# mLSTM gate rows on 32 partitions, worked out beside GLA, in a hybrid mixer kernel

## The chip, the cores and the metric

The kernel runs on one core of a Trainium2 chip. The metric is the device time of one execution in microseconds, taken as the median of several executions. TensorE (PE) multiplies, VectorE (DVE) and GpSimd (POOL) work elementwise, ScalarE (ACT) does functions and casts, and SyncE (SP) issues nearly all DMAs. Each engine works through its own instructions in order and waits on semaphores for the others.

## The reference, cut to what matters

The whole program is a hybrid mixer block (three branches: GLA, mLSTM and S5, then a merge and a SwiGLU feed-forward) followed by an MLA and RG-LRU block, for 1024 tokens of width 1024 in float32. The change touches the gates of the mLSTM branch:

```python
def mlstm_memory(q, k, v, i_pre, f_pre):
    log_f = jax.nn.log_sigmoid(f_pre.astype(f32))
    ...
        b = jnp.cumsum(lfi, axis=-1)                      # inside a chunk
        a_inter = b + m_prev[..., None]
        d_intra = jnp.where(causal, b[..., :, None] - b[..., None, :] + ii[..., None, :], -jnp.inf)
        m_t = jnp.maximum(a_inter, jnp.max(d_intra, axis=-1))
        w_inter = jnp.exp(a_inter - m_t)
        scores = jnp.einsum('bhtd,bhsd->bhts', qi, ki) * jnp.exp(d_intra - m_t[..., None])
        ...
        h = num / jnp.maximum(jnp.abs(den), jnp.exp(-m_t))[..., None]
        w_key = jnp.exp(b[..., -1:] - b + ii - m_new[..., None])
```

There are 4 heads of key width 64 and value width 128, and the mixer also holds `y_gla = rms_norm(o_gla) * silu(gr)`, `y_ml = sigmoid(mo) * h_ml` and `y_s5 * sigmoid(y_s5 @ s5_glu_w + s5_glu_b)`, whose products stand next to the change in the program. Six rows of modulation come from `silu(c) @ ada_w + ada_b`.

## The kernel before, in words

Every float32 product is split into a high and a low part and done as three matmuls (`mm3`), with operands of 128 rows and 256 or 512 columns. Weights come by one DMA (`wr`), a cast on ACT (`wh`) and a difference on DVE (`wl`). `e()` gives one of four general 128x1028 buffers: loads, gate results and stores all pass through these four. PSUM tiles are `psg` (big products) and `psc` (small ones).

Code is written as generators that yield an estimated delay. A small driver (`spawn`, `push`, `drive`) runs them by a clock of its own and so fixes the order in which instructions are written; after that a scheduler with a timeline of its own reorders them on each engine. Pools lie on two stacks of the on-chip memory, left and right. Where a pool is opened on space that another one has left, each new tile waits for the last users of whatever tile lay there before (`reuse_waits="tile"`).

The order around the change is this:

- GLA stage: `gla_pair` for two pairs of heads runs beside the products `in_ml` (mLSTM's q and k, written to `d_mq`) and `in_v(1)` (its v). `ada_rest` is not yet there in program order, but the scheduler moves its first loads and sums forward into this stage.
- Gate rows: `ml_rows` loads the pre-activations of the gates as two 4x1024 tiles, `mr_i` and `mr_f` (one partition for each head, all 1024 steps along it), and makes from them log-sigmoid, sums inside a chunk, the running maximum by one scan over 1024 steps, and the rows that the mLSTM needs, in two 128x1024 tiles printed as `r`. `ml_core` transposes one of them in 8 pieces to columns (`becol`, `wkcol`, `encol`) and exponentiates two; `sel` is a matrix that picks a row and spreads it over 128 partitions.
- mLSTM stage: `ml_core` works in four blocks (two pairs of heads, two halves of the time). A block loads q, k, v (one buffer each), spreads the gate rows by `r,sel` and a mask `mneg`, takes `D` by Exp, and does `q,k`, `v,kT`, `Sz,qt` and `v,P` and the transposes of `P`. Beside it run `in_gr` (the GLA gate, `psg<-ah,wh` and so on), `s5_glu` (loads `e<-d_sy`, eight DMAs for each of four pieces, cast to `gh`, low part `gl`, and products `gh,wh` and so on), `in_mo`, and `proj(2)`.
- `ada_rest` goes through eight groups. A group clears the accumulator `ada0` on POOL, loads a piece of bias into it, then for 8 weights loads one (three buffers `ada1` to `ada3`) and adds it on DVE, sums over partitions with a matmul by `ones`, and stores a row to `d_rows`.
- Projections: `load_yb` loads a branch's output and splits it in `yb0` (high, ACT) and `yb1` (low, DVE); `proj` makes eight 128x1024 tiles, copied out of `psg` by ACT (`e<-psg`) and stored to `d_p`. `proj(0)` asks at its sixth tile for the load of `proj(1)`'s operand, into a pool `yb2` that is opened after mLSTM and `ada_rest` have ended, on the space that they leave.

Of the kernel before, what the change touches and what calls it, by code (L numbers as in the profile page):

```python
# [51 lines left out]
class Kernel:  # L52
# [1105 lines left out]
    def ml_rows(self, p):  # L1158

        nc = self.nc  # L1160
        t = lambda n: p.tile([4, 1024], F32, name="mr_" + n)
        r1 = self.mrow.tile([128, 1024], F32, name="r1")
        r2 = self.mrow.tile([128, 1024], F32R, name="r2")
        nc.gpsimd.memset(r1, 0.0)
        nc.gpsimd.memset(r2.bitcast(F32), 0.0)
        f, i, a = t("f"), t("i"), t("a")
        nc.sync.dma_start(i, self.d_misc[32:36])
        nc.sync.dma_start(f, self.d_misc[64:68])
        self.ts(i, i, self.co["ifb"][0:4, 0:1], op0=ALU.add)
        self.ts(f, f, self.co["ifb"][0:4, 1:2], op0=ALU.add)  # L1170
        self.log_sigmoid(a, f)
        b, m = t("b"), a
        self.local_sums(b, f, 4)
        nc.vector.tensor_tensor_scan(out=m, data0=f, data1=i, initial=0.0, op0=ALU.add, op1=ALU.max)
        m_be, m_ka, m_nm = r1[0:4], r1[32:36], r1[64:68]
        self.m_cols, self.m_rows = r1, r2
        c8 = lambda x: x.rearrange("p (c n) -> p c n", c=8)
        m_a, aw = t("ma"), f
        self.tt(m_a, b, m, ALU.subtract)
        self.tt(m_be, i, b, ALU.subtract)  # L1180
        self.ts(m_nm, m, -1.0)
        nc.vector.tensor_copy(aw[:, 0:128], m_a[:, 0:128])
        self.tt(c8(aw)[:, 1:], c8(m_a)[:, 1:],
                c8(m)[:, 0:7, 127:128].to_broadcast([4, 7, 128]), ALU.add)
        self.tt(c8(m_ka), c8(m_be), c8(m_a)[:, :, 127:128].to_broadcast([4, 8, 128]), ALU.add)

        for o, x in ((0, m_a), (64, aw)):
            h = p.tile([4, 1024], F32R, tag="mr_h", name="mr_h")
            nc.vector.tensor_copy(h, x)
            self.tt(r2[o + 32:o + 36], x, h.bitcast(F32), ALU.subtract)  # L1190
            nc.scalar.copy(r2[o:o + 4], h.bitcast(F32))

    def ml_core(self, p1, p2):
        nc, A = self.nc, self.A
        sel = p1.tile([128, 6, 128], F32R, name="sel")
# [3 lines left out]
        for o in (0, 32, 64, 96):  # L1199
            nc.sync.dma_start(sf[o:o + 4], sv)  # L1200
        nc.gpsimd.tensor_copy(sel, sf)
        yield 16.0

        be = p1.tile([128, 8, 4], F32, name="becol")
        wk = p1.tile([128, 8, 4], F32, name="wkcol")
        en = p1.tile([128, 8, 4], F32, name="encol")
        for g in range(2):
            pcol = self.psc()
            for c in range(4):
                self.tr(pcol[:, c * 128:c * 128 + 128], self.m_cols[:, (4 * g + c) * 128:(4 * g + c) * 128 + 128])  # L1210
            pv = pcol.rearrange("p (c n) -> p c n", c=4)
            cs = slice(4 * g, 4 * g + 4)
            nc.vector.tensor_copy(be[:, cs], pv[:, :, 0:4])
            self.act(wk[:, cs], pv[:, :, 32:36], AF.Exp)
            self.act(en[:, cs], pv[:, :, 64:68], AF.Exp)
# [5 lines left out]
        for pr in range(2):  # L1221
            nc.gpsimd.memset(Sz, 0.0)
            for u in range(2):
# [10 lines left out]
                for hh, r, _ in heads:  # L1234
                    hd = 2 * pr + hh
                    pdm = self.psc()
                    self.mm(pdm, sel[0:64, hd], self.m_rows[0:64, ts_], True, False)
                    D = t2("D", [128, 512])
                    for c in range(4):
                        s = slice(c * 128, c * 128 + 128)  # L1240
                        self.mm(pdm[:, s], self.identb, self.mneg[:, 256:384], False, c == 3)
                    for c in range(4):
                        s = slice(c * 128, c * 128 + 128)
                        self.act(D[:, s], pdm[:, s], AF.Exp, bias=be[:, 4 * u + c, hd:hd + 1])
                    Ds.append(D)
# [11 lines left out]
                for c in range(4):  # L1257
                    for hh in range(2):
                        self.ts(kT[:, c, hh], kp[:, c, hh],
                                wk[:, 4 * u + c, 2 * pr + hh:2 * pr + hh + 1], 0.125, ALU.mult, ALU.mult)  # L1260
                yield 3.0
# [17 lines left out]
                yield 6.4  # L1279
                for c in range(4):  # L1280
# [7 lines left out]
                    self.stt(den, O[:, :, 128], -1.0, en[:, 4 * u + c, 2 * pr:2 * pr + 2], ALU.mult, ALU.max)  # L1288
# [4 lines left out]
                    yield 0.5  # L1293
# [1115 lines left out]
    def main(self):  # L2409
        A = self.A  # L2410
        W = lambda i: (A["w_ws"][i], 1024)
        with ExitStack() as sec:
# [5 lines left out]
            with ExitStack() as es:  # L2418
# [15 lines left out]
                yield from self.join(*hbs)  # L2434
            with ExitStack() as es:
# [9 lines left out]
                yield from self.join(*gl)  # L2445
# [95 lines left out]
def _prep(**a):  # L2541
# [3 lines left out]
    o = {}  # L2545
# [69 lines left out]
    ifb[0:4, 0] = a["ml_i_b"][0]  # L2615
    ifb[0:4, 1] = a["ml_f_b"][0]
# [63 lines left out]
```

## Time and profile before

| | |
|---|---|
| median of 3 executions | 2783.6 us (2775.06 to 2789.24) |
| profiled execution, its own time | 2771.37 us |
| its span in the trace | 2769.6 us |
| busy: PE, DVE, ACT, POOL | 95%, 64%, 37%, 28% of the span |
| mean granted clock of TensorE | 0.981 of full |

PE is busy nearly all the time, and most of the span is a chain of matmuls. What a change can win or lose stands in the few places where PE waits, and these are found by stage. In rows of the trace a start and a duration are given, then engine, line, operation and operands, and in brackets how long the engine was idle before and what released it.

### The profile page before, as it was taken

What the parts mean: (1) busy time and instruction counts of PE and PEld (TensorE: products, weight loads), DVE (VectorE), ACT (ScalarE), POOL (GpSimd) and SP (SyncE); (2) the same over time, 40 slices, a digit from 0 to 9 for tenths busy, and PEclk for the clock granted to TensorE, in tenths of its full rate; (3) what the DMA queues carried; (4) which work ended last, traced back from release to release, by engine and by line L of the source; (5) the groups of instructions that cost most, each with busy time, mean ns of one, the idle gap of its engine ahead of it and who ended that gap; (6) DMA issues with size and microseconds to landing.
All of it is one profiled execution on the core that took longest, in us unless ns stands there. A gap on an engine that the chain in (4) does not pass through costs nothing. (4 is left out here: it accounts for less than half of the span.)

```text
span 2769.6 us, 40630 instructions
## 1 busy us (share of the span) xinstructions
PE 2640.8 (95%) x15928; PEld 2173.1 (78%) x15928; DVE 1761.5 (64%) x2668; ACT 1036.8 (37%) x1590; POOL 763.4 (28%) x563
## 2 busy tenths in 40 slices
PE   6999899998999999999999999999989998999998
PEld 4788687776788899888989788787766665976688
DVE  7785855655776766644444466644577767667676
ACT  6564535322433446422222311231433344146330
POOL 4221110000244502344444000321315546123332
PEclk8999999999999999999999999999999999999999
DMA  8334315567433364222221422333220114322231
GB/s 250 111 93 151 119 54 166 188 210 265 153 104 109 115 206 145 80 81 84 77 92 69 160 91 95 133 115 94 79 77 26 35 45 156 111 70 71 67 115 62
DMA packets 143084, 313.08 MB, mean 113 GB/s; under 512 B 20910, under 2 KB 64766, under 8 KB 142764
## 3 DMA queue, kind: packets, MB, share of 16 engines
q1 hardware_dynamic: 142892, 310.48, 33.5%
q8 instruction: 126, 2.06, 0.3%
q14 instruction: 66, 0.54, 0.1%
HBM read 228.84 MB, written 80.23 MB: 112 GB/s over the span
## 5 line engine op out<-in xcount | busy, mean ns | idle before, releaser
L120 PE MATMUL psg<-ah,wh 128*128 128x512 f32 x1104 | 444.9, 404 | 12.4 <-ACT ah L421 8.7
L120 PE MATMUL psg<-al,wh 128*128 128x512 f32 x1104 | 439.6, 398 | 2.1 <-DVE al L136 2.0
L120 PE MATMUL psg<-ah,wl 128*128 128x512 f32 x1104 | 439.6, 398 | 0.0
L136 DVE TENSOR_TENSOR wl<-wr,wh 128x1024 fp32r<-128x1024 f32 (+3 forms) x208 | 272.1, 1309 | 239.0 <-ACT wh L1506 114.7
L179 ACT CAST wh<-wr 128x1024 fp32r<-128x1024 f32 (+3 forms) x133 | 133.0, 1002 | 487.0 <-PE psg L120 210.2
L120 PEld LDWEIGHTS psg<-ah,wh 128*128 128x128 f32 x1104 | 208.9, 190 | 67.2 <-issue 10.7
L120 PE MATMUL psc<-wh,ah 128*128 128x256 f32 x896 | 252.3, 283 | 2.1 <-DVE mx L136 1.0
L120 PEld LDWEIGHTS psg<-al,wh 128*128 128x128 f32 x1104 | 209.4, 190 | 54.6 <-issue 5.6
L120 PE MATMUL psc<-wl,ah 128*128 128x256 f32 x896 | 249.4, 279 | 2.1 <-issue 1.5
L120 PE MATMUL psc<-wh,al 128*128 128x256 f32 x896 | 248.7, 279 | 0.0
L120 PEld LDWEIGHTS psg<-ah,wl 128*128 128x128 f32 x1104 | 209.5, 190 | 47.9 <-issue 2.8
L136 DVE TENSOR_TENSOR e<-psc,e 128x512 f32<-128x512 f32 (+1 forms) x210 | 138.2, 673 | 133.6 <-PE psc L120 133.2
L120 PE MATMUL psc<-tx,wh 128*128 128x256 f32 x1056 | 190.1, 281 | 3.3 <-DVE e L136 3.3
L136 POOL TENSOR_TENSOR e<-e 128x1024 f32<-128x1024 f32 (+3 forms) x65 | 108.8, 1677 | 242.8 <-ACT e L148 122.9
L120 PEld LDWEIGHTS psc<-wh,ah 128*128 128x128 f32 x896 | 170.1, 190 | 6.3 <-ACT wh L179 1.7
L120 PEld LDWEIGHTS psc<-wl,ah 128*128 128x128 f32 x896 | 170.2, 190 | 2.8 <-issue 1.7
L120 PEld LDWEIGHTS psc<-tx,wh 128*128 128x128 f32 x1056 | 165.2, 189 | 6.8 <-issue 3.5
L120 PEld LDWEIGHTS psc<-wh,al 128*128 128x128 f32 x896 | 169.8, 190 | 0.1
L136 POOL TENSOR_TENSOR acc<-acc,e 128x512 f32<-128x512 f32 (+2 forms) x60 | 116.6, 1943 | 159.2 <-PE psc L120 141.2
L120 PE MATMUL psc<-tx,wl 128*128 128x256 f32 x528 | 147.9, 280 | 0.0
L120 PE MATMUL psc<-ah,wh 128*128 128x512 f32 (+1 forms) x368 | 143.4, 393 | 3.0 <-ACT ystore L148 2.0
L120 PE MATMUL psc<-al,wh 128*128 128x512 f32 (+1 forms) x368 | 143.3, 389 | 1.5 <-DVE al L136 1.5
(513 smaller groups left out, 5915.9 us busy)
## 6 DMA issues: line engine op xcount, KB each, us to landing
wr<-in_w_ws_dram SPq DMA_DIRECT2D x45, 512.0 KB
wr<-in_ffn_in_dram SPq DMA_DIRECT2D x44, 512.0 KB
ada<-in_ada_w_dram SPq DMA_DIRECT2D x64, 256.0 KB
d_p<-e SPq DMA_DIRECT2D x24, 512.0 KB
e<-d_p SPq DMA_DIRECT2D x24, 512.0 KB
wr<-in_w_out_dram SPq DMA_DIRECT2D x24, 512.0 KB
d_h<-e SPq DMA_DIRECT2D x22, 512.0 KB
wr<-in_ffn_out_dram SPq DMA_DIRECT2D x22, 512.0 KB
```

What stands on the lines that cost most here:

```text
L120: self.nc.tensor.matmul(out, lhsT, rhs, start=start, stop=stop)
L136: (eng or self.nc.vector).tensor_tensor(out=out, in0=a, in1=b, op=op)
L179: (self.nc.vector.tensor_copy if self.hi_dve else self.nc.scalar.copy)(hi[:, :n], raw[:, :n])
```

## The change

`ml_rows` becomes a generator that is spawned beside GLA, 12 us after GLA's inputs are ready. It holds the gates as 32x128 tiles (head and chunk on partitions), so that one instruction covers 128 steps instead of 1024. The running maximum is first taken inside each chunk; then the last columns of 32 partitions are moved to one row by two small matmuls, four scans of 8 steps run over the chunks of each head, and one matmul moves the result back to a column of 32. The columns come from one 128x128 transpose, and the rows reach their places in `mr_rows` through DRAM (one store, four loads). `sel` is built here too. The pool `mrow` lies now on the right stack, from the GLA stage to the end of mLSTM. `ml_core` takes `sel`, rows and columns over, and the delays that it yields are a little larger.

```diff
-        t = lambda n: p.tile([4, 1024], F32, name="mr_" + n)
-        r1 = self.mrow.tile([128, 1024], F32, name="r1")
-        r2 = self.mrow.tile([128, 1024], F32R, name="r2")
...
-        self.local_sums(b, f, 4)
-        nc.vector.tensor_tensor_scan(out=m, data0=f, data1=i, initial=0.0, op0=ALU.add, op1=ALU.max)
...
+        t = lambda n, w=128: p.tile([32, w], F32, name="mr_" + n)
+        cols = p.tile([128, 128], F32, name="mr_cols")
+        rows = p.tile([128, 1024], F32R, name="mr_rows")
+        sel = p.tile([128, 6, 128], F32R, name="sel")
...
+        yield 6.0
+        self.ts(i, i, self.co["ifb"][0:32, 0:1], op0=ALU.add)
+        self.ts(f, f, self.co["ifb"][0:32, 1:2], op0=ALU.add)
+        self.log_sigmoid(a, f)
+        yield 4.0
+        nc.vector.tensor_tensor_scan(out=b, data0=self.ones[0:32], data1=f, initial=0.0, op0=ALU.mult, op1=ALU.add)
+        nc.vector.tensor_tensor_scan(out=x, data0=f, data1=i, initial=-1e30, op0=ALU.add, op1=ALU.max)
+        yield 4.0
+        ps = self.psc()
+        for n, v in enumerate((b, x)):
+            self.mm(ps[0:1, 32 * n:32 * n + 32], v[:, 127:128], self.ident[0:32, 0:32], True, True)
+        me = p.tile([1, 64], F32, name="mr_me")
+        nc.vector.tensor_copy(me, ps[0:1, 0:64])
+        for h in range(4):
+            nc.vector.tensor_tensor_scan(out=mp[:, h, 1:9], data0=me[:, 8 * h:8 * h + 8],
+                                         data1=me[:, 32 + 8 * h:40 + 8 * h], initial=0.0, op0=ALU.add, op1=ALU.max)
...
+        self.mm(ps[0:32, 0:1], mc, self.ones[0:1, 0:1], True, True)
+        prev = t("prev", 1)
+        nc.vector.tensor_copy(prev, ps[0:32, 0:1])
+        self.stt(m, b, prev, x, ALU.add, ALU.max)
...
+        nc.sync.dma_start(d.rearrange("g h (c n) -> (g h c) n", c=8), hl.bitcast(F32))
+        for g in range(4):
+            nc.sync.dma_start(rows[32 * g:32 * g + 4].bitcast(F32), d[g])
+        yield 6.0
+        self.tr(ps[:, 0:128], cols)
...
+            eM = ExitStack()
+            mrow = self.pool("mrow", es=eM, side="right")
...
+                rows = self.spawn(self.ml_rows(mrow), 12.0)
...
-                    self.mrow = self.pool("mrow", es=e2)
-                    with ExitStack() as e3:
-                        self.ml_rows(self.pool("mlr", es=e3))
+                    e2.enter_context(eM)
```

The change moves instructions at three places. On PE, at the end of `in_gr` (the rows `psg<-ah` and `psg<-al`), before:

```order
L120 MATMUL psg<-ah,wl 128x512
L120 MATMUL psc<-r_4998,sel 128x512
L120 LDWEIGHTS identb
L120 MATMUL psc<-mneg,identb 128x128
...
L120 MATMUL psc<-r_4998,sel 128x512
L127 MATMUL psc<-ident,k 128x128 x4
L120 MATMUL psc<-q,k 128x128 x8
L120 MATMUL psc<-v,kT 128x258 x4
L120 MATMUL psc<-Sz,qt 128x258
L120 MATMUL psc<-v,P 128x129 x2
L120 MATMUL psg<-gh,wh 128x512 x2
```

And the end of `in_gr` in the changed kernel:

```order
L120 MATMUL psc<-mr_rows,sel 128x512
L120 MATMUL psg<-ah,wl 128x512
L127 MATMUL psc<-ident,k 128x128 x4
L120 MATMUL psg<-ah,wh 128x512
L120 MATMUL psc<-q,k 128x128 x8
L120 MATMUL psg<-al,wh 128x512
L120 MATMUL psg<-ah,wl 128x512
L120 MATMUL psc<-v,kT 128x258 x4
L120 MATMUL psc<-Sz,qt 128x258
L120 MATMUL psc<-v,P 128x129 x2
L120 MATMUL psc<-Sz,qt 128x258
```

Before, the first block of mLSTM comes behind the last matmul of `in_gr`; in the changed kernel the first block and the second up to its `q,k` are spread between the matmuls of `in_gr`, and what is shown is the second block.

On SP, at the same place, where q, k and v of mLSTM and the pieces `e<-d_sy` of `s5_glu` are loaded, before:

```order
L176 DMA wr<-in_proj_dram 128x1024
L628 DMA d_y<-e 128x1024
L1226 DMA q<-d_mq 128x512
L1227 DMA k<-d_mq 128x512
L1229 DMA v<-d_v 128x2x128 x4
L834 DMA e<-d_sy 16x8x128 x6
L628 DMA d_y<-e 128x1024
L834 DMA e<-d_sy 16x8x128 x3
L1227 DMA k<-d_mq 128x512
L834 DMA e<-d_sy 16x8x128
L1226 DMA q<-d_mq 128x512
L834 DMA e<-d_sy 16x8x128 x12
```

And in the changed kernel:

```order
L1247 DMA v<-d_v 128x2x128 x2
L628 DMA d_y<-e 128x1024
L1247 DMA v<-d_v 128x2x128 x2
L1320 DMA d_y<-y 128x512 x2
L1244 DMA q<-d_mq 128x512
L834 DMA e<-d_sy 16x8x128 x10
L628 DMA d_y<-e 128x1024
L834 DMA e<-d_sy 16x8x128 x22
```

The q shown last is that of the third block; it has moved ahead of all 32 loads `e<-d_sy`, and it goes into the buffer that the second block's `q,k` on PE still reads.

On DVE, at the end of `proj(0)`, the eighth group of `ada_rest` and the low parts `yb` of `proj(1)`'s operand, before:

```order
L136 TENSOR_TENSOR yb_6961<-e,yb_6960 128x1024
L145 SCALAR_TENSOR_TENSOR e<-e 128x1024
L145 SCALAR_TENSOR_TENSOR ada_5047<-ada_5050,cact,ada_5047 128x512
L145 SCALAR_TENSOR_TENSOR ada_5047<-ada_5048,cact,ada_5047 128x512
L136 TENSOR_TENSOR yb_6961<-e,yb_6960 128x1024
L145 SCALAR_TENSOR_TENSOR ada_5047<-ada_5049,cact,ada_5047 128x512
L145 SCALAR_TENSOR_TENSOR ada_5047<-ada_5050,cact,ada_5047 128x512
L145 SCALAR_TENSOR_TENSOR ada_5047<-ada_5048,cact,ada_5047 128x512
```

And in the changed kernel:

```order
L145 SCALAR_TENSOR_TENSOR ada_5072<-ada_5074,cact,ada_5072 128x512
L145 SCALAR_TENSOR_TENSOR ada_5072<-ada_5075,cact,ada_5072 128x512
L145 SCALAR_TENSOR_TENSOR ada_5072<-ada_5073,cact,ada_5072 128x512
L145 SCALAR_TENSOR_TENSOR ada_5072<-psc,ada_5074 1x512
L136 TENSOR_TENSOR yb_6959<-e,yb_6958 128x1024 x3
L145 SCALAR_TENSOR_TENSOR e<-e 128x1024
L136 TENSOR_TENSOR yb_6959<-e,yb_6958 128x1024
```

All four low parts have moved behind the whole eighth group. The first of them waits there for the DMA that stores `ada0` to `d_rows`, and before it waited for ACT only: without `mrow` and `sel` on the left stack, the pool `yb2` now begins on the space where `ada0` lay.

## Rows read from the trace of the kernel before

**Rows 1.** Windows: busy us (instructions) of PE, PEld, DVE, ACT, POOL; clock, DMA share, GB/s.
```profile
285.00:335.00 50.00, 39.40 (x750) 31.40 (x738) 46.82 (x110) 24.55 (x42) 3.47 (x4) 0.88 0.31 102
465.00:502.00 37.00, 27.68 (x139) 20.74 (x139) 26.35 (x66) 21.31 (x34) 2.10 (x4) 0.86 0.68 192
```

**Rows 2.** Timeline of DVE, the row chain, first and last instruction and two scans.
```profile
440.61 0.74 DVE L140 TENSOR_SCALAR mr_i<-mr_i,cols 4x1024 f32<-4x1024 f32 x1 [3.24 <-DMA mr_i<-d_misc]
...
448.66 1.21 DVE L145 SCALAR_TENSOR_TENSOR mr_f<-mr_f,mr_a 4x1024 f32<-4x1024 f32 x1 [3.13 <-ACT mr_a L148]
449.91 2.62 DVE L560 TENSOR_TENSOR_SCAN mr_b<-ones,mr_f 4x128 f32<-4x128 f32 x8
...
466.51 0.26 DVE L1213 COPY becol<-psc 128x16 f32<-128x16 f32 x2
```

**Rows 3.** Timeline of PE from GLA's end through the first mLSTM blocks.
```profile
429.49 0.48 PE L120 MATMUL psg<-ah,wh 128*128 128x512 f32 x1
...
464.64 0.40 PE L120 MATMUL psg<-ah,wl 128*128 128x512 f32 x1
467.35 0.50 PE L120 MATMUL psc<-r,sel 64*128 64x512 f32 x1 [2.31 <-POOL sel L1201]
...
473.71 3.11 PE L120 MATMUL psc<-q,k 64*128 64x128 f32 x16 [3.68 <-ACT D L148]
...
483.53 0.60 PE L120 MATMUL psc<-Sz,qt 128*128 128x258 f32 x2
...
491.84 2.08 PE L120 MATMUL psc<-q,k 64*128 64x128 f32 x16
...
499.51 0.74 PE L120 MATMUL psg<-gh,wh 128*128 128x512 f32 x2 [1.24 <-ACT gh L845]
```

**Rows 4.** Timeline of all engines: S5 loads (SP), cast (ACT) and low part (DVE).
```profile
478.19 5.63 SPq L834 DMA_DIRECT2D e<-d_sy  x12
...
497.52 1.94 ACT L845 CAST gh<-e 128x1024 fp32r<-128x1024 f32 x1 [2.44 <-DMA e<-d_sy]
...
499.49 1.96 DVE L136 TENSOR_TENSOR gl<-e,gh 128x1024 fp32r<-128x1024 f32 x1 [1.07 <-ACT gh L845]
```

**Rows 5.** Groups by line on DVE, 262 to 335 us: busy, mean ns | idle before.
```profile
L145 DVE SCALAR_TENSOR_TENSOR ada<-ada,cact,ada 128x512 f32<-128x512 f32 x8 | 6.0, 747 | 0.0
...
L136 DVE TENSOR_TENSOR mx<-psc,mD 128x128 f32<-128x128 f32 x20 | 5.4, 282 | 0.0
```

**Rows 6.** Timeline of ACT in the row chain.
```profile
446.28 1.28 ACT L148 ACT_TABLE_LOAD   x1
```

**Rows 7.** Timeline of PE at the end of `proj(0)`.
```profile
687.91 0.40 PE L120 MATMUL psg<-yb,wl 128*128 128x512 f32 x1
696.96 1.22 PE L120 MATMUL psg<-yb,wh 128*128 128x512 f32 x2 [8.65 <-ACT e L886]
```

**Rows 8.** The eight stores of `d_rows` by tile: ns min/median/max, first and last start.
```profile
L348 SPq DMA_DIRECT2D d_rows<-ada x8: 235/242/642, 551.6 to 718.5; - x8
```

**Rows 9.** Timeline of SP and POOL: four of these stores, and clearing `ada0` after two.
```profile
578.40 0.24 SPq L348 DMA_DIRECT2D d_rows<-ada  x1
...
579.63 0.53 POOL L331 MEMSET ada<- 128x512 f32 x1 [24.74 <-DMA d_rows<-ada]
...
596.70 0.64 SPq L348 DMA_DIRECT2D d_rows<-ada  x1
...
687.78 0.24 SPq L348 DMA_DIRECT2D d_rows<-ada  x1
...
693.44 0.52 POOL L331 MEMSET ada<- 128x512 f32 x1 [27.11 <-DMA d_rows<-ada]
...
718.48 0.24 SPq L348 DMA_DIRECT2D d_rows<-ada  x1
```

**Rows 10.** Timeline of ACT and DVE before PE resumes in `proj(0)`.
```profile
695.90 1.00 ACT L886 COPY e<-psg 128x1024 f32<-128x1024 f32 x1
...
696.02 1.23 DVE L136 TENSOR_TENSOR yb<-e,yb 128x1024 fp32r<-128x1024 f32 x1 [1.11 <-ACT yb L1461]
```

More of the change, by code (lines that the diff above doesn't have):

```diff
@@ L1181, in ml_rows @@
[L1181 to L1191, printed above, removed]
@@ L1193, in ml_core @@
-    def ml_core(self, p1, p2):
-        nc, A = self.nc, self.A
-        sel = p1.tile([128, 6, 128], F32R, name="sel")
+        nc, A = self.nc, self.A
+        t = lambda n, w=128: p.tile([32, w], F32, name="mr_" + n)
+        cols = p.tile([128, 128], F32, name="mr_cols")
+        hl = p.tile([128, 128], F32R, name="mr_hl")
+        rows = p.tile([128, 1024], F32R, name="mr_rows")
+        sel = p.tile([128, 6, 128], F32R, name="sel")
+        mp = p.tile([1, 4, 9], F32, name="mr_mp")
+        self.m_col = p.tile([128, 3, 4, 8], F32, name="mr_col")
@@ L1196, in ml_core @@
+        d = self.drp.tile([4, 4, 1024], F32, name="d_mr")
+        f, i, a, b, x, m = [t(n) for n in "fiabxm"]
+        nc.sync.dma_start(i, self.d_misc[32:36].rearrange("h (c n) -> (h c) n", c=8))
+        nc.sync.dma_start(f, self.d_misc[64:68].rearrange("h (c n) -> (h c) n", c=8))
         sf = self.e()[:, 0:768].rearrange("p (a n) -> p a n", a=6)
@@ L1200, in ml_core @@
             nc.sync.dma_start(sf[o:o + 4], sv)
+        nc.gpsimd.memset(rows.bitcast(F32), 0.0)
+        nc.gpsimd.memset(cols, 0.0)
+        nc.gpsimd.memset(mp, 0.0)
         nc.gpsimd.tensor_copy(sel, sf)
[L1202 to L1215, printed above, removed]
+        yield 6.0
@@ new lines, in ml_rows @@
+        me = p.tile([1, 64], F32, name="mr_me")
[3 more added lines that the diff above has]
+                                         data1=me[:, 32 + 8 * h:40 + 8 * h], initial=0.0, op0=ALU.add, op1=ALU.max)
+        mc = p.tile([1, 32], F32, name="mr_mc")
+        nc.vector.tensor_copy(mc.rearrange("p (h c) -> p h c", h=4), mp[:, :, 0:8])
+        yield 4.0
+        ps = self.psc()
@@ new lines, in ml_rows @@
+        self.mm(ps[0:32, 0:1], mc, self.ones[0:1, 0:1], True, True)
+        prev = t("prev", 1)
+        nc.vector.tensor_copy(prev, ps[0:32, 0:1])
+        self.stt(m, b, prev, x, ALU.add, ALU.max)
+        self.tt(x, b, m, ALU.subtract)
+        self.tt(cols[0:32], i, b, ALU.subtract)
+        self.ts(cols[32:64], cols[0:32], x[:, 127:128], op0=ALU.add)
+        self.ts(cols[64:96], m, -1.0)
+        self.ts(a, x, prev, op0=ALU.add)
+        for o, v in ((0, x), (64, a)):
+            nc.scalar.copy(hl[o:o + 32], v)
+            nc.scalar.copy(f, hl[o:o + 32].bitcast(F32))
+            self.tt(hl[o + 32:o + 64], v, f, ALU.subtract)
@@ new lines, in ml_rows @@
+        nc.sync.dma_start(d.rearrange("g h (c n) -> (g h c) n", c=8), hl.bitcast(F32))
+        for g in range(4):
+            nc.sync.dma_start(rows[32 * g:32 * g + 4].bitcast(F32), d[g])
+        yield 6.0
+        ps = self.psc()
+        self.tr(ps[:, 0:128], cols)
+        pv = ps[:, 0:96].rearrange("p (x h c) -> p x h c", x=3, h=4)
+        nc.vector.tensor_copy(self.m_col[:, 0], pv[:, 0])
+        self.act(self.m_col[:, 1:3], pv[:, 1:3], AF.Exp)
+        self.m_rows, self.m_sel = rows, sel
@@ L1216, in ml_core @@
+    def ml_core(self, p1, p2):
+        nc, A = self.nc, self.A
+        sel = self.m_sel
+        be, wk, en = [self.m_col[:, x] for x in range(3)]
+        yield 8.0
         Sz = p1.tile([128, 5, 2, 129], F32, name="Sz")
@@ L1243, in ml_core @@
                         s = slice(c * 128, c * 128 + 128)
-                        self.act(D[:, s], pdm[:, s], AF.Exp, bias=be[:, 4 * u + c, hd:hd + 1])
+                        self.act(D[:, s], pdm[:, s], AF.Exp, bias=be[:, hd, 4 * u + c:4 * u + c + 1])
                     Ds.append(D)
@@ L1259, in ml_core @@
                         self.ts(kT[:, c, hh], kp[:, c, hh],
-                                wk[:, 4 * u + c, 2 * pr + hh:2 * pr + hh + 1], 0.125, ALU.mult, ALU.mult)
-                yield 3.0
+                                wk[:, 2 * pr + hh, 4 * u + c:4 * u + c + 1], 0.125, ALU.mult, ALU.mult)
+                yield 4.5
                 P = t1("P", [128, 2, 4, 128])
@@ L1278, in ml_core @@
                                  ALU.mult, ALU.add)
-                yield 6.4
+                yield 7.5
                 for c in range(4):
@@ L1292, in ml_core @@
                         self.ts(P[:, hh, c], O[:, hh, 0:128], den[:, hh:hh + 1])
-                    yield 0.5
+                    yield 0.7
                 yield 3.0
@@ L2442, in main @@
                 self.finish(ready)
+                rows = self.spawn(self.ml_rows(mrow), 12.0)
                 yield from self.in_ml()
                 yield from self.in_v(1)
-                yield from self.join(*gl)
+                yield from self.join(*gl, rows)
             with ExitStack() as es:
@@ L2614, in _prep @@
     ifb = z0(128, 2)
-    ifb[0:4, 0] = a["ml_i_b"][0]
-    ifb[0:4, 1] = a["ml_f_b"][0]
+    ifb[0:32, 0] = np.repeat(a["ml_i_b"][0], 8)
+    ifb[0:32, 1] = np.repeat(a["ml_f_b"][0], 8)
     cc = {
```

18 lines of the change are left out of this document (1 added, 17 removed).

## The prediction

> **What bounds the kernel now.** PE is busy for 95% of the span, so a change is worth what it takes from or adds to the places where PE waits. I read the windows by stage first, and in the stages that the change touches the timelines. Three places matter.
>
> In the GLA stage PE is not the bound: between 285 and 335 us DVE is busy for 46.82 of 50 us and PE for 39.40, at a granted clock of 0.88 [rows 1]. What is added to DVE there is paid in time.
>
> After GLA, PE runs through `in_gr` without a gap, from 429.49 to 464.64 [rows 3], while the row chain goes through DVE: 21 lines of the timeline from 440.61 to 466.51 [rows 2], one of which waits 3.13 us for ACT. When the matmuls of `in_gr` are used up, the chain is not done. PE waits 2.31 us for `sel`, and 3.68 us for `D` [rows 3], and for S5's operands: the cast `gh` waits for the loads `e<-d_sy` (2.44 us), and PE 1.24 us for `gh` [rows 3, 4]. In the window of 37 us from 465 to 502, PE is busy 27.68 us at a granted clock of 0.86 [rows 1]. This is the loss that the change can address.
>
> At the end of `proj(0)` PE stops from 688.3 to 696.96, for 8.65 us, for a copy on ACT [rows 7]. The copy needs a free buffer of the four `e`, and these hold the inputs from which DVE makes the low parts `yb` of the next operand.
>
> **The change, part by part.** The sum is made against the profiled execution, 2771.4 us; the median of the runs, 2783.6, lies 12.2 above it, and I carry differences over to the median unchanged.
>
> *The mLSTM stage.* The row chain leaves DVE's queue here, and the mLSTM's first block and the second up to its `q,k` now lie between the matmuls of `in_gr`. A block on PE, by the rows: three spreads with two sets of masks, about 2.0 (0.50 each [rows 3] and the masks between); transposes of k 0.5; `q,k` 2.08 [rows 3]; `v,kT` about 2.1; four readouts at 0.88, half the distance between readouts in the timeline from 483.53 on being one, 3.5; transposes of `P` 1.0. That is 11.2. 150 matmuls of `in_gr` are left at 429.49, at 35.15/153 or 0.229 each (464.64 less 429.49) [rows 3]: 34.3. So PE has done `in_gr`, the first block and 4.6 of the second at 429.5 + 34.3 + 11.2 + 4.6 = 479.6.
>
> Here comes a new wait. SP has the third block's q ahead of all 32 loads `e<-d_sy`; q has one buffer, and the second block's `q,k` is PE's next to last piece before 479.6. So the loads, which before were spread from 467 on between other work, start at 479.6. Twelve took 5.63 [rows 4], 32 take about 15; with 2 to 3 for landing, a cast of 1.94 and a low part of 1.96 [rows 4], the last low part is there at about 501, and its matmuls end at about 501.7. Before, the last low part was there at 501.45 (499.49 + 1.96 [rows 4]), and its matmuls ended about 502.4. So S5 gains only 0.7. But mLSTM is then further by about 5.5 us (four readouts of the second block, its transposes, and part of the third's rows), which fill PE's waits. Of the 6.2 I take off 1.5 for PE's restarts at half clock while it waits for the loads piece by piece, and add 1 for waits for `kT` that fall away: **5.7 gained**. Bounds: 1, if PE stands still for the loads and the third block cannot fill; 11, if all idle time of the window (37 less 27.68) [rows 1] and some of the clock's loss comes back.
>
> *The GLA stage.* Out go the eight sums of `ada` that stood in this window on DVE, 6.0 us [rows 5]; they move to the time of `in_gr`, where the row chain has made room. In come 23 small operations on 32 partitions. None is in the trace; the nearest are `mx`, 128x128 out of PSUM, 0.28 [rows 5], and a copy of 16 columns, two in 0.26 [rows 2]. So 3.0 to 6.4, and I take 4.6, and 0.6 for two scans of 128 steps, eight of which took 2.62 [rows 2]. log-sigmoid makes DVE's next operation wait for Exp and Ln on ACT, with a table load of 1.28 each [rows 6]; before, that wait was 3.13 [rows 2]. I take 2.3 (0 to 3.1), the functions being eight times shorter. Behind it on DVE are GLA's `mx` and `d`, for which PE waits. Net: 4.6 + 0.6 + 2.3 - 6.0 = **1.5 lost** (3 gained to 5 lost). The trip of the rows through DRAM, five DMAs on SP, and the clearing on POOL lie beside GLA, which runs on to 429.49 [rows 3]; that cover hides them, and without it they would stand ahead of the first spread as the row chain did.
>
> The trace shows 1.28 for the load and 1.29 from its start to the function behind it [rows 6]. By the Trainium skill, "ScalarE: Activation LUTs", section "What ACT_TABLE_LOAD costs", a switch of sets costs 2.66, with a drain beside the load. By that the GLA stage would lose 2.8 more; the timeline shows no such time, and the row stands.
>
> *The projections.* What the change frees on the left stack moves everything above it. The pool `yb2` now begins over the accumulator `ada0`, so that DVE's first low part of `yb1` waits until `ada_rest` is through: eight sums, the matmul, the row, and the landing of its store. In the changed order all four low parts stand behind the eighth group. Behind the low parts are the four `e`, behind these ACT's copies of `proj(0)`'s tiles, and behind these PE. The groups are 23.8 apart on average (8 stores from 551.6 to 718.5 [rows 8]), the shortest 18.3 (578.40 to 596.70), the last 30.7 (687.78 to 718.48) [rows 9]. In the last one the matmul waited nearly 5 us in PE's queue behind `proj(1)`, and its loads were behind two stores; without both it would be about 21.5. A store takes from 1.23 (578.40 to 579.63) to 5.66 us (687.78 to 693.44) to land [rows 9]; 3.6 is the middle. The seventh store was at 687.78; in the changed order it has one low part of `yb` less ahead of it, so 686.8. Then PE resumes at 686.8 + 21.5 + 3.6 + two low parts, 2.4, + one copy, 1.05 [rows 10] = 715.4, and not at 696.96: **18.4 lost** (13.5 with 18.3 and a short landing, 23 with the mean and a long one). Nothing hides it: PE has nothing else in its queue there. The gain of the stages ahead moves the groups with it, since each waits for its matmul in PE's order.
>
> A landing counts once here, behind the last store. By the Trainium skill, "DMA: Bandwidth & Descriptors", the section on one DMA's anatomy, a DMA has a fixed cost of about 2 us, most of it the receipt of the write; the rows show both less and nearly three times that. By the page's figure this term would be 1.6 smaller.
>
> **Sum:** 1.5 - 5.7 + 18.4 = +14.2, that is 2785.6 against the profiled 2771.4, and **2797.8** against the median.
>
> **The rivals.** (1) *The group is early enough; not slower.* The wait for `ada0` costs nothing from the point where the eighth store lands before 693, when the first low part was due. That needs the groups 18 us earlier. For it: one group's loads and matmul less would do, and the changed order has the last matmul by `ones` ahead of `proj(0)`'s last 24. Against it: each group waits for its predecessor's landing and its own loads, and the first matmul stands at the same place as before. Then only the stages count: -4.2, or 2779.4, and down to 2770 if the mLSTM stage gains its bound of 11 and GLA loses nothing. (2) *Both at their good ends:* the mLSTM stage gains 11, the wait is 13.5: +4, 2787.6. For it speak the 9.3 us of PE's idle time [rows 1]; against it that S5's loads begin late. (3) *GLA pays.* The chunks' maximum goes from DVE to PE, back, to PE and back; if each of the three hops stalls DVE or PE by as much as the 3.13 for ACT [rows 2], 9 come on top: +23, 2807. For it: DVE is full there [rows 1]; against: the chain has all of GLA, to 429 [rows 3], to finish in. (4) *It doesn't do what it says.* The loads behind the third q cost as much as the rows' chain did, and the stage gains nothing: +20, 2803.5.
>
> **How the numbers follow.** The forecast has 0.40; (1) 0.18, (2) 0.15, (3) 0.14, (4) 0.13. A measurement of this kernel tells about 0.5%, or 13.9 us, from no change, and the forecast lies on that bound, half on either side. Slower by more: 0.20 + 0.14 + 0.13 = 0.47. Within: 0.20 + 0.15 + half of (1), 0.09 = 0.44. Faster by more: the other half of (1), where the runs' own scatter adds: 0.09. The range runs from (1), 2779, to the wait's upper bound with little gain ahead, +26, 2810. What is left out is the lower part of (1) and the upper of (3).
>
> **What would show it.** In the profile after: `r,sel` (now `mr_rows,sel`) between the matmuls of `in_gr`, no wait for `sel`; loads `e<-d_sy` not before about 479; a stop of PE of some 27 us near 690, ended by ACT's copy, with `yb` on DVE waiting for `d_rows<-ada`; DVE fuller than before between 285 and 335. The prediction is wrong if that stop is no longer than before, or if GLA's end moves by more than 5 us.

## The result, and the profile after

The changed kernel takes 2793.6 us in the median of 19 executions (2782.1 to 2802.8), the kernel before 2779.9 in as many (2769.3 to 2789.6). The ratio is 1.0052, with a 95% interval from 1.0038 to 1.0066: 14.5 us slower, and 14.2 had been forecast. The range, 2779 to 2810, held it. But the sum came out right with two of its three terms wrong, and in opposite directions, which is luck. The rows below show it, and the experiments show where the time went.

The profiled execution of the changed kernel took 2798.5 us, a second one 2798.4, both some 5 us above the medians; the two profiles of the kernel before took 2771.4 and 2775.9, 4 to 8 below theirs. So traces of the two kernels lie 23 to 27 us apart where medians lie 14 apart. I read from them in which stage time goes, and take sizes of the whole from the medians.

Windows of the changed kernel (columns as in [rows 1]):

```profile
285.00:335.00 50.00, 43.52 (x770) 34.71 (x770) 43.77 (x116) 24.96 (x45) 3.34 (x2) 0.83 0.25 83
335.00:430.00 95.00, 85.03 (x1339) 78.50 (x1339) 54.77 (x152) 38.40 (x118) 16.35 (x30) 0.91 0.19 63
465.00:502.00 37.00, 35.13 (x179) 28.54 (x178) 23.78 (x67) 12.41 (x18) 0.89 (x2) 0.96 0.55 178
478.40:515.40 37.00, 29.75 (x144) 21.27 (x142) 20.08 (x54) 21.22 (x31) 1.23 (x2) 0.92 0.56 171
```

And one of the kernel before:

```profile
335.00:430.00 95.00, 90.09 (x1432) 83.42 (x1432) 51.29 (x147) 41.45 (x129) 18.98 (x36) 0.99 0.20 69
```

The window from 465 to 502 is what the change was to repair. PE is busy there for 35.13 us where it was 27.68 [rows 1], but the changed kernel is 13.4 us late by then (next rows) and still has matmuls of `in_gr` in this window. The window that holds the same work, 478.4 to 515.4, has 29.75 us at a granted clock of 0.92, against 27.68 at 0.86: the stage is repaired in part. In the GLA stage PE is granted less: 0.83 against 0.88 between 285 and 335 [rows 1], and 0.91 against 0.99 from 335 to 430. At the two levels, full and half clock, that is 17 and 17 us at half clock; the kernel before has 12 and 2. The second profiles give 30 us in all (0.83 and 0.93) against 13 (0.95 and 0.96).

The timeline of PE, GLA's last transposes, the first matmul of `in_gr` behind them, and the end of `proj(0)`:

```profile
442.12 1.03 PE L127 MATMUL psc<-ident,P 128*128 128x128 f32 x8
442.91 0.48 PE L120 MATMUL psg<-ah,wh 128*128 128x512 f32 x1
...
698.38 0.40 PE L120 MATMUL psg<-yb,wl 128*128 128x512 f32 x1
715.45 1.87 PE L120 MATMUL psc<-ada,ones 128*1 128x512 f32 x2 [16.66 <-DVE ada L145]
722.80 1.22 PE L120 MATMUL psg<-yb,wh 128*128 128x512 f32 x2 [5.49 <-ACT e L886]
```

The matmul at 442.91 answers to that at 429.49 [rows 3]: by it PE has done the same number of matmuls of each big kind in both kernels, and it comes 13.4 us later, of which 1.3 were there before the stage began (the same matmul stands at 262.21 and 263.46). The stop at the end of `proj(0)` is two now, 16.66 and 5.49 us, where it was one of 8.65 [rows 7].

To see where time goes in all runs, I follow PE's work: each matmul counted at its usual distance, and the time at which the same work is done, against the second profile of the kernel before, set to zero at 262 us. Positive is later. Marks are times of the kernel before: 430 is GLA's end, 560 lies behind S5 and mLSTM's third block, 685 and 760 before and behind the stop at `proj(0)`.

| profile | 430 | 560 | 685 | 760 | 1100 |
|---|---|---|---|---|---|
| before (first) | -0.5 | -1.8 | -2.9 | -8.1 | -8.4 |
| after (first) | 11.2 | 6.2 | 6.8 | 15.0 | 18.7 |
| after_again | 9.3 | 5.0 | 4.5 | 12.6 | 17.9 |
| after_pad | 9.7 | 6.2 | 4.7 | 11.8 | 11.9 |
| after_pad_pool | 10.8 | 5.7 | 3.2 | 5.1 | 8.5 |
| before_shift | 1.4 | -0.4 | -5.1 | 8.7 | 13.3 |
| before_shift_pad | -0.5 | -1.9 | -6.5 | 4.6 | 5.6 |
| before_shift_right | -1.1 | -3.4 | -8.3 | -5.7 | -3.2 |
| after_ada_right | 9.5 | 5.4 | 6.8 | 9.2 | 9.4 |
| ada_right_late | 0.9 | -4.3 | -5.4 | -3.9 | -5.6 |
| ada_right_nohop | 6.0 | 2.3 | -1.4 | -0.2 | 2.5 |
| ada_right_late_qk | 1.8 | -5.1 | -3.8 | -9.5 | -9.7 |
| late_qk_again | 1.4 | -7.2 | -4.8 | -11.0 | -9.3 |

Two profiles of one kernel differ by up to 2 us at 430 and up to 8 at 760, so a single entry is known no better than that. Behind 1100 us single profiles drift against one another by 5 us and more either way, two profiles of one kernel too.

### The profile page after: what moved, and what is told of

It reads as the page before. It is cut to its first block, busy times and chain, and to the rows that moved or that the text cites. A ratio compares the mean times of both kernels' runs of the same rounds, so it can differ in the third digit from the quotient of the medians.

```text
span 2796.6 us, 40632 instructions
## 1 busy us (share of the span) xinstructions
PE 2652.6 (95%) x15927; PEld 2179.4 (78%) x15927; DVE 1749.2 (63%) x2665; ACT 1036.2 (37%) x1590; POOL 762.3 (27%) x564
```

## The experiments

Two theories stood at first. A: the new wait at `proj(0)` makes the change slower, as the prediction had it. B: the gate rows cost their time in the GLA stage.

**A pad under `ada0`.**

```diff
+                    pa.tile([128, 256], F32, name="pad")
                     sa = [pa.tile([128, 512], F32, name="ada%d" % i) for i in range(4)]
```

> The changed kernel with 1 KB of unused memory put below the accumulator ada0, so that the pool yb2 no longer lies over it; nothing else moves. Theory A, the new wait is what makes the change slower: PE's stop at the end of proj(0) falls from 27 us in all to 9 or less, and the time by 13 to 18 us against the changed kernel, to 2776 to 2781 (0.998 to 1.000 of before). Theory B, the loss is the gate rows in the GLA stage, and the stop only shows it late: the stop gets shorter, but the time falls by no more than 5 us, to 2788 or above (1.003 or more of before).

Measured: 2791.2 us, 1.0043 of before (1.0026 to 1.0059). The time is what theory B had, but neither theory had the stop: it is 22.3 us in two waits, where the changed kernel has 22.2. PE's waits from 680 to 760 us in the padded kernel:

```profile
PE psc L120 <- DVE ada L145: 18.2, 1, 18.2
PE psg L120 <- ACT e L886: 4.1, 1, 4.1
```

The semaphore is gone: DVE's first low part, which in the changed kernel waits for the store of `ada0`, no longer does. First the changed kernel, then the padded one:

```profile
717.35 0.68 DVE L145 SCALAR_TENSOR_TENSOR ada<-psc,ada 1x512 f32<-1x512 f32 x1 [1.96 <-PE psc L120]
719.29 3.50 DVE L136 TENSOR_TENSOR yb<-e,yb 128x1024 fp32r<-128x1024 f32 x3 [1.27 <-DMA d_rows<-ada]
```

```profile
715.37 0.68 DVE L145 SCALAR_TENSOR_TENSOR ada<-psc,ada 1x512 f32<-1x512 f32 x1 [1.96 <-PE psc L120]
715.98 3.47 DVE L136 TENSOR_TENSOR yb<-e,yb 128x1024 fp32r<-128x1024 f32 x3
```

It was worth 1.3 us. PE stops all the same, since in its written order the last matmul by `ones` still stands ahead of `proj(0)`'s last 24, and DVE's low parts still stand behind the sums. So the order holds PE and not the semaphore; what made the order was open.

**The memory map alone, old row chain.**

```diff
-                    self.mrow = self.pool("mrow", es=e2)
+                    self.mrow = self.pool("mrow", es=e2, side="right")
...
-        sel = p1.tile([128, 6, 128], F32R, name="sel")
+        sel = self.mrow.tile([128, 6, 128], F32R, name="sel")
```

> The kernel before with the change's memory map alone: mrow and sel on the right stack, the row chain and everything else as before. ada0 then lies under yb2, and the first group of ada_rest can't start in the GLA stage. Theory A: slower by the new wait alone, 13 to 18 us, 2793 to 2798 (1.005 to 1.0065 of before), with a stop of 20 us or more at the end of proj(0). Theory B: at most 3 us slower, 2783 or below, since the row chain hasn't moved into GLA.

Measured: 2787.0 us, 1.0039 of before (1.0023 to 1.0055), 10.9 us by the ratio; between the two theories and nearer to A. PE's waits from 680 to 760 (in all, how many, the longest):

```profile
PE psc L120 <- DVE ada L145: 22.1, 2, 13.2
PE psg L120 <- ACT e L886: 5.5, 1, 5.5
```

The stop is there without any of the new rows. Moving 11 KB to the other stack is enough for it. And at 430 the kernel is 1.4 us late in the table and not early, although the first eight sums of `ada_rest` have left the GLA stage here too: they had cost nothing there.

**The map and the pad.**

> The kernel of the run before this one with 1 KB of unused memory below ada0: old row chain, mrow and sel on the right, the first group of ada_rest out of the GLA stage, no wait of yb on ada0. Theory A: within 5 us of before, 2775 to 2785; less than before by up to 5 us if the eight sums of ada_rest stood on the path of the GLA stage, as the prediction has it. Against the padded changed kernel it shows the rows alone: theory A expects it 2 to 6 us slower than that one (row chain on the path), theory B 5 us or more faster than that one (no row work in GLA).

This is the kernel above with the pad of the first run. Measured: 2791.2 us, 1.0043 (1.0021 to 1.0064), so not the 2775 to 2785 of theory A: the pad does nothing here either. At 430 it is level with before (-0.5), against 9.7 of the padded changed kernel. That is theory B's part: the rows cost GLA 10 us in these two profiles. But the whole time, where theory B had this kernel 5 us or more faster than the padded changed one, is the same for both (1.0043). Some of it goes at `proj(0)`, where PE's stops are 25.2 us here and 22.3 there, but the table still has 7 us between the two at 760; where the medians lose these is not shown.

**The changed kernel again.**

> The changed kernel as it is, for a second profile. The time is 2794 (2789 to 2799), 1.004 to 1.007 of before. Theory B: GLA's last transposes of P again stand 10 us or more later than before (442 against 429), with some 30 us at half clock between 285 and 430. Theory A: they stand there by chance of the one profile, and now come 2 to 6 us later than before, at 431 to 435; and matmuls between 740 and 1000 are 0.229 apart as before, not 0.233.

Measured: 2791.9 us, 1.0056 (1.0038 to 1.0073). GLA's end is again 9.3 us late, so it is no chance of one profile, and the matmuls between 740 and 1000 are again 0.233 apart. So theory B has GLA's end right, and theory A, with the order in place of the semaphore, the stop at `proj(0)`. Each is a part.

**The pool of `ada_rest` on the right stack.**

```diff
-                    pa = self.pool("ada", es=e2)
+                    pa = self.pool("ada", es=e2, side="right")
```

> The changed kernel with the pool of ada_rest on the right stack, above mrow, one word changed. The padded run showed that the wait of yb on ada0 is not what stops PE: without it the last matmul by ones still stands ahead of proj(0)'s end in PE's order, and PE waits 18 us for it. With the pool on the right the written order is again as before: this matmul stands among proj(1)'s, and the low parts yb between the sums of the eighth group. Theory C, the order is the cause: the stop falls from 22 us to 9 or less, the time by 11 to 15 us against the changed kernel, to 2777 to 2782 (0.999 to 1.002 of before). If memory or the stores of d_rows are the cause in another way, the stop stays above 15 us and the time above 2788.

Measured: 2789.7 us, 1.0032 (1.0012 to 1.0052). The direction is right and the size too large: the gain over the changed kernel is about 6 us by the ratios, not 11 to 15, and the stop is 14.4 us, not 9. PE's waits from 680 to 760:

```profile
PE psg L120 <- ACT e L886: 14.4, 2, 10.0
```

The stop for `ada` is gone. What is left are two waits for ACT's copies, 10.0 and 4.4. The second profile of the kernel before has them as well, 13.3 in all, and the first had only 9.6. So of the 18.4 us that I had put on the new wait, 8 to 9 are left against the second profile and 13 against the first.

**The gate rows later in GLA.**

```diff
-                rows = self.spawn(self.ml_rows(mrow), 12.0)
+                rows = self.spawn(self.ml_rows(mrow), 100.0)
```

> The same with the gate rows spawned 100 us after GLA's inputs are ready, not 12, so that their small operations stand in GLA's second half, where DVE is busy for half the time. Three profiles show that at equal work PE is 10 us behind at GLA's end with the rows in the first half. Theory D, the rows' operations and hops stand on the path there: GLA's end comes 7 to 10 us earlier than in the run before this one and the time falls as much, to 2768 to 2775 (0.996 to 0.999 of before). If the 10 us come from elsewhere (the stores, the clearing on POOL, memory moved), GLA's end stays and the time is within 3 us of the run before this one.

Measured: 2780.9 us, 1.0012 (0.9991 to 1.0033). GLA's end comes 8.6 us earlier than in the run before (0.9 against 9.5), as expected; of the time, some 5.6 by the ratios, so that it lies above the 2768 to 2775 expected. The windows of this kernel:

```profile
285.00:335.00 50.00, 40.12 (x715) 31.64 (x714) 47.10 (x115) 24.57 (x46) 4.40 (x5) 0.90 0.26 87
335.00:430.00 95.00, 88.17 (x1420) 81.67 (x1419) 50.59 (x153) 41.31 (x129) 18.11 (x34) 0.98 0.21 70
```

The granted clock is back at 0.90 and 0.98, that is 10 and 4 us at half clock. The edit moved only a part of the rows, though. On DVE, the end of log-sigmoid, and the first and last copy of the part behind it:

```profile
274.85 0.28 DVE L145 SCALAR_TENSOR_TENSOR mr_f<-mr_f,mr_a 32x128 f32<-32x128 f32 x1
358.79 0.20 DVE L1196 COPY mr_me<-psc 1x64 f32<-1x64 f32 x1
368.96 0.18 DVE L1225 COPY mr_col<-psc 128x32 f32<-128x32 f32 x1
```

Log-sigmoid with its table load and the two scans over 128 steps are still at GLA's start, where the scheduler has moved them, 1 to 6 us later than in the run with the pool on the right. From the hops on the operations come 61 to 69 us later than there, and cost nearly nothing. So most of the loss goes with the hops and what follows them; log-sigmoid at GLA's start costs little.

**No way from chunk to chunk.**

```diff
-        for n, v in enumerate((b, x)):
-            self.mm(ps[0:1, 32 * n:32 * n + 32], v[:, 127:128], self.ident[0:32, 0:32], True, True)
...
-        self.mm(ps[0:32, 0:1], mc, self.ones[0:1, 0:1], True, True)
         prev = t("prev", 1)
-        nc.vector.tensor_copy(prev, ps[0:32, 0:1])
+        nc.gpsimd.memset(prev, 0.0)
```

> The same as the first of these runs, rows at 12 us, but without the way of the running maximum from chunk to chunk: the three small matmuls, the four scans of 8 and three copies are left out (the maximum that a chunk begins with is zero), so it leaves out part of the computation. Rival 3 of the prediction, the hops between DVE and PE stall GLA: its end comes 6 us or more earlier than with them, and the time falls by that. If the other 15 operations of the rows and the two table loads in DVE's full stretch are the cause, it comes at most 3 us earlier.

Measured: GLA's end 3.5 us earlier (6.0 against 9.5), between the two answers. Without the hops the operations behind them move forward too, from 300 to 308 us to 270 to 279, all but the transpose and its copies, so the run can't part them; that the hops carry a third of GLA's loss would be a guess. What it does show is where the 3.5 us came from: PE's waits in the stage are no shorter (18.5 us against 17.7), but it is 21 us at half clock (granted 0.90 and 0.94 in the two windows) and not 30 (0.83 and 0.93). The whole, 2769.9 us, 0.9977 (0.9953 to 1.0000), fell by more than the stage accounts for, and I don't build on that.

**The kernel before again.**

> The kernel before as it is, for a second profile. The first one (2771) was 8 us below the median of the runs of before (2780). Whether the 26 us between the two first profiles are the change or the scatter: if scatter, this profile is 5 us or more above the first one and the difference lies outside the stretch from 262 to 760 us; if not, it is within 3 us of the first up to there.

Measured: 2775.9 us in the profiled execution, 4.5 above the first. It is within 3 us of the first up to 685, and then loses 5.2 between 685 and 760, since its stop is two waits of 9.3 and 4.0 us and the first's was 8.65 and 0.91. So the scatter is there, but inside the stretch and not outside it. The stop is thus not the same in each execution, and the price of the new one depends on which it is held against: 13.4 us by the first profile (8.2 less -5.2), 8.2 by the second.

**Third q and k on another queue.**

```diff
-                nc.sync.dma_start(q, self.d_mq[pr][:, ts_])
-                nc.sync.dma_start(k, self.d_mq[2 + pr][:, ts_])
+                qk = nc.gpsimd if pr and not u else nc.sync
+                qk.dma_start(q, self.d_mq[pr][:, ts_])
+                qk.dma_start(k, self.d_mq[2 + pr][:, ts_])
```

> The changed kernel with the pool of ada_rest on the right, the rows spawned at 100, and the third block's q and k loaded from POOL's queue, not SP's, so that the 32 loads e<-d_sy no longer stand behind the wait for the second block's q,k. The prediction said that these loads start only with that q,k. If that wait is what S5 loses, the loads start 6 to 8 us earlier against the rest of the program, PE's wait for gh and gl (4 us in the changed kernel) goes, and the time falls by 4 to 8 us against the run with late rows, to 2773 to 2777. If the loads are late for another reason, or mLSTM can't fill what S5 leaves, within 2 us of it.

Measured: 2772.5 us, 0.9991 (0.9976 to 1.0005), some 6 us less than with late rows alone by the ratios of two batches. SP, first with late rows, then with this edit too:

```profile
471.81 0.82 SPq L1320 DMA_DIRECT2D d_y<-y  x2
479.76 0.32 SPq L1244 DMA_DIRECT2D q<-d_mq  x1
480.13 4.68 SPq L834 DMA_DIRECT2D e<-d_sy  x10
485.25 0.34 SPq L628 DMA_DIRECT2D d_y<-e  x1
485.64 11.00 SPq L834 DMA_DIRECT2D e<-d_sy  x22
```

```profile
475.00 0.82 SPq L1321 DMA_DIRECT2D d_y<-y  x2
475.88 4.78 SPq L834 DMA_DIRECT2D e<-d_sy  x10
488.45 0.34 SPq L628 DMA_DIRECT2D d_y<-e  x1
488.83 10.80 SPq L834 DMA_DIRECT2D e<-d_sy  x22
```

The wait for q was real: the first ten loads go out 0.1 us behind the stores and not 7.5. But the other 22 now wait for the last tile of `in_gr`, `d_y<-e`, until 488.45; the next instruction in the queue takes the place of the one removed. PE's waits for `gh` (2.9 us in the kernel with late rows) are gone all the same. In the table the stage gains 1.7 (from 1.8 to -5.1, against 0.9 to -4.3), and the rest of the 6 us is not in it.

**The old row chain with the same map.**

> The kernel before with mrow, sel and the pool of ada_rest on the right stack: old row chain behind GLA, written order of projections as before, first group of ada_rest out of GLA. Against after_ada_right, which has the same memory map, it shows the gate rows alone. By the traces the rows cost 10 us in GLA and give 4 to 5 back in the mLSTM stage: this run is then 4 to 8 us faster than after_ada_right (2790), 2782 to 2786. By the prediction's terms (1.5 lost or, without the eight sums, 7.5 lost, 5.7 gained) it would be 2 us faster to 4 us slower, 2788 to 2794. Against before it also shows whether the map costs anything by itself: within 4 us, or the wait at proj(0) is back in another form.

Measured: 2778.9 us, 1.0010 (0.9994 to 1.0027); the time lies under the 2782 to 2786 expected. Against after_ada_right (1.0032), in another batch, the new rows at 12 us cost about 6 us by the ratios, which is what the traces had led to; the prediction's own terms would have had them at 2 us gained to 4 lost. By itself the map costs some 3 us by the ratio, and 7 at the interval's end, when `ada0`'s pool lies on the right. But the written order is not that of before. PE's waits from 680 to 760:

```profile
PE psc L120 <- DVE ada L145: 11.3, 2, 8.4
PE psg L120 <- ACT e L886: 3.2, 1, 3.2
```

The matmul by `ones` of the seventh group stands ahead of `proj(0)`'s last 24 here, though `yb2` does not lie over its pool, and PE waits 8.4 us for it; the eighth stands among `proj(1)`'s. In all PE waits 14.5 us, as in after_ada_right. So the overlap can account for the place of the eighth group, and that of the seventh in this kernel has another cause, which stays open.

**The pad as a pool of its own.**

```diff
+                    self.pool("pad", es=e2).tile([128, 256], F32, name="pad")
                     pa = self.pool("ada", es=e2)
```

> The changed kernel with the 1 KB of unused memory as a pool of its own below the pool of ada_rest, not as a tile inside it. In the first padded run yb2 still lay over the edge of that pool, though over none of its used tiles, and the written order stayed. With the pad outside, the written order is again that of before: the last matmul by ones among proj(1)'s matmuls, the low parts between the sums. If the scheduler's order follows from two pools lying over each other, and that order is what stops PE, the stop falls from 22 us to 15 or less over the two waits for ACT's copies, and the time is that of the run with the pool on the right, 1.002 to 1.004 of before. If the right stack brought the gain there in another way, it stays at 1.0045 or more.

Measured: 2787.0 us, 1.0035 (1.0021 to 1.0048). PE's waits from 680 to 760:

```profile
PE psg L120 <- ACT e L886: 13.6, 2, 9.1
```

This is as expected, and it settles the cause of the order in the changed kernel. With the same 1 KB outside the pool and not within it, the eighth group's matmul by `ones` stands among `proj(1)`'s again, and the stop for `ada` goes. The scheduler orders by pools that lie over each other, also where no tile in use does; the semaphore follows the tiles.

**All three repairs again.**

> The kernel with all three repairs once more, as it is, on another chip's terms: pool of ada_rest on the right, rows late, third q and k on POOL's queue. 0.997 to 1.001 of before, as in its first run (0.9991, 0.9976 to 1.0005). If the map, GLA's waits and S5's loads were the whole of the loss, the prediction's gain of the mLSTM stage remains, some 4 to 6 us (0.998); if something else of the change costs time after 760 us, it is 1.000 or more.

Measured: 2771.0 us, 0.9976 (0.9958 to 0.9993). With its first run (0.9991) that is a kernel 0.1 to 0.24% faster than the one before, 2.5 to 6.7 us, and 0.6 to 0.8% faster than the changed one; the interval of the first run still holds no change at all. The 5.7 us forecast for the mLSTM stage lie between the two, but that this gain is the edit's own is not shown: with its rows late and the pool on the right, but q and k left on SP, the kernel was no faster than before (1.0012).

## Why the prediction was right, and where it was not

*The GLA stage: the step that failed.* The sum had 1.5 us lost, with bounds from 3 gained to 5 lost; it was 9.3 to 11.2, outside, and the prediction itself had named a move of GLA's end by more than 5 us as a sign of being wrong. The operations were sized well: they take 5.4 us on DVE, where 4.6 and 0.6 were taken, and DVE waited 2.00 for ACT's log-sigmoid, where 2.3 was taken (the first rows of DVE's timeline below). Nor was DVE fuller than before, as the prediction had it: 43.77 us between 285 and 335, against 46.82. Two other things were wrong. First, I let the eight sums of `ada_rest` give back 6.0 because DVE was busy for 46.82 of 50 us [rows 1, 5]. Three runs in which they leave the stage, and nothing comes in, end it at 1.4, -0.5 and -1.1. So the sums had cost nothing where they stood: a full engine doesn't mean that each thing in it is on the path. Second, the rows stand in a chain with PE and ACT, and PE's share of that, its stops and its clock, was priced at nothing in the sum (rival 3 had the stops):

```profile
269.50 0.27 DVE L145 SCALAR_TENSOR_TENSOR mr_a<-mr_f 32x128 f32<-32x128 f32 x1
271.77 0.28 DVE L145 SCALAR_TENSOR_TENSOR mr_f<-mr_f,mr_a 32x128 f32<-32x128 f32 x1 [2.00 <-ACT mr_a L148]
272.08 0.41 DVE L1189 TENSOR_TENSOR_SCAN mr_b<-ones,mr_f 32x128 f32<-32x128 f32 x1
...
285.19 0.43 DVE L136 TENSOR_TENSOR d<-q,d 128x256 f32<-128x256 f32 x1 [2.72 <-ACT d L148]
...
288.63 0.20 DVE L1196 COPY mr_me<-psc 1x64 f32<-1x64 f32 x1
```

```profile
284.36 0.22 PE L120 MATMUL psc<-ident,mr_x 32*1 32x32 f32 x2
286.89 0.46 PE L120 MATMUL psc<-d 64*32 64x32 f32 x32 [2.32 <-DVE d L136]
...
304.16 0.33 PE L127 MATMUL psc<-ident,mr_cols 128*128 128x128 f32 x1
306.76 1.05 PE L120 MATMUL psc<-d 64*32 64x32 f32 x96 [1.46 <-ACT mr_col L148]
```

DVE's copy comes 4 us behind the matmul that it waits on, and PE waits 1.46 for the Exp of `mr_col`. The 2.32 just behind the first hop are not the hop's: DVE's `d` had itself waited 2.72 for ACT, and the run without hops has a wait of 2.45 us at the same place (286.90). PE's waits in the stage are only 2.5 us more in all than before (17.8 against 15.3). The rest is the clock: 34 us at half of it and not 14, so at most 10 us of work lost. The stops come at other places, and more of the time behind them is granted half the clock. Waits and clock together, worked out in this way, give 12.5 us for the changed kernel, 7 for the run without hops and 1.5 for late rows (16.7 of waits), where the table has 11.2, 6.0 and 0.9. That the moved stops brought the clock down is read from this agreement; no run changed the clock alone.

*The mLSTM stage: right, a little too large.* 5.7 gained was forecast, with bounds of 1 and 11; from 430 to 560 the two profiles gain 5.0 and 4.3, and those of before 1.3 and 0 against each other, so 3 to 5. The mechanism is as told, and the waits for `sel` and `D`, 2.31 and 3.68 before, are gone. PE has the second block's `q,k` at 490.38, and the loads come behind it:

```profile
492.12 0.32 SPq L1244 DMA_DIRECT2D q<-d_mq  x1
492.49 5.27 SPq L834 DMA_DIRECT2D e<-d_sy  x10
```

Less the 13.4 us that GLA ends later, 492.5 is 479.1, where 479.6 was forecast. PE waits for `gh` at most 2.73 us, against 1.24 [rows 3], and that takes a part of the gain back.

*The projections: right place and order, wrong size and half a wrong reason.* The wait that I named, the store of `ada0`, is 1.27 us; the rest of what the change adds comes from the order which the overlap of the pools brings about, and the pad outside the pool shows it. In the prediction I gave the order as a consequence of that wait and summed along it, so that most of the sum held: the eighth group took 21.47 us from store to store (696.59 to 718.06), and 21.5 was taken. The landing was 1.23, at the lower bound, and not 3.6. Against that the stop of before is larger than the one profile showed: 13.3 us in the second. Together that makes 18.4 into 8 to 13. Two bounds were slips on which nothing hangs: with 18.3 and a landing of 1.23 the terms give 12.8 and not 13.5, and the low end of rival 1 is 2772.6 (2783.6 less 11) and not 2770.

*The sum.* 1.5 became 10, 5.7 became 3 to 5, and 18.4 became 8 to 13: 13 to 20, where 14.2 was forecast and 14.5 measured. These sizes are from single profiles, which lie 23 to 27 us apart, and the wider matmuls of the last section add some 5 us in both profiles of the changed kernel; against the medians the account does not close better than that. The size of rival 3, GLA pays, came true, and its reason, hops that stall PE, at best in part; it would have given 23 with the wait as forecast, and the smaller wait hid it. So the time was right by two errors that cancel, and that is luck; the forecast's bounds for GLA were the worst part of it.

*Beside the Trainium skill.* By the Trainium skill, "ScalarE: Activation LUTs", section "What ACT_TABLE_LOAD costs", with a drain beside each load, GLA would have lost 2.8 more. The wait for log-sigmoid was 2.00 with one load of 1.28 in it, so the trace doesn't show such a drain, and the stage's loss came from elsewhere. The landing of 1.23 here is under the 2 us of the Trainium skill, "DMA: Bandwidth & Descriptors", section "Anatomy of one DMA", as the shortest row had shown; the section gives that figure for DMAs issued by GpSimd, and these stores are issued by SP.

## What to carry to other kernels

A pool that is moved off a stack moves every later pool, and in this program the scheduler reordered PE and DVE where two pools came to overlap, even by 1 KB with no tile in use; look at the written order of both kernels, and put the pad or the pool elsewhere before the edit is judged. Work taken off a full engine gives time back only if something waited behind it, and work put on it as a chain across engines can cost more than its own duration: here 9 to 11 us for 5.4 us of operations, most of it in time that PE spent at half clock. A transfer queue in order passes a wait on: with q gone from SP, the next store held 22 of the same 32 loads. A window at a fixed time compares the same work only if nothing ahead of it has moved; and before a run with a changed delay is read, look which instructions moved.

## What the runs showed of the hardware

Between about 728 and 1010 us the changed kernel's 512-column matmuls are 0.233 us apart at a granted clock of 1.00, where those of before are 0.229. Behind the stop the timeline of the changed kernel reads:

```profile
824.00 0.40 PE L120 MATMUL psc<-al,wh 128*128 128x512 f32 x1
824.24 0.40 PE L120 MATMUL psc<-ah,wl 128*128 128x512 f32 x1
824.47 0.40 PE L120 MATMUL psc<-ah,wh 128*128 128x512 f32 x1
824.70 0.40 PE L120 MATMUL psc<-al,wh 128*128 128x512 f32 x1
```

Over these 280 us that is 5 us, with PE never idle (15.0 at 760 to 18.9 at 960 in its lag). Both profiles of the changed kernel, before_shift and after_pad_pool have it; the padded ones, and all that have the pool on the right, have 0.229 nearly throughout. It is no effect of the long stop (after_pad stops as long and hasn't it, after_pad_pool has it without), and from 760 to 1010 the changed kernel and after_pad have the same matmuls in the same order, by names and shapes; where the tiles lie in memory the traces don't show, and no run tested it. I have no cause for it; it stays open.
